# Three modulation vectors a stage later, three by column-group products on TensorE

## The chip, the cores and the metric

One core of one Trainium2 chip runs the whole program. The metric is device time in microseconds (us) of one execution. The engines are TensorE (PE in the profile, its weight loads PEld), VectorE (DVE), ScalarE (ACT), GpSimd (POOL) and the SyncE queue (SP), which issues most transfers.

## The reference, cut to what matters

Two layers of a hybrid backbone run over two streams of 256 tokens each: the latent stream (stream 1 in the kernel) and the context stream (stream 0). Every layer has a SwiGLU FFN, a token mixer of four branches, and a second FFN. Each of these sub-layers is wrapped in a norm with shift, scale and gate vectors, and those are nine columns of 1024 out of one product per layer and stream:

```
mod_l = (act_l @ w_mod[i] + b_mod[i])          # act_l = silu(c),     latent
mod_c = (act_c @ w_mod[i][:, :n_c] + ...)      # act_c = silu(c_ctx), context; last layer: 5 of 9
xl = ffn_sublayer(xl, ml, 0, ...); hl = modulated_norm(xl, g[2], ml[3], ml[4])
xl = xl + ml[5] * rms_norm(yl, g[3]); xl = ffn_sublayer(xl, ml, 6, ...)
```

A modulation vector is a product of one activation row of 1024 with a 1024 x 1024 matrix, 4 MB of weights in float32. Vectors are numbered j = 0 to 8; 0 to 2 belong to the first FFN, 3 to 5 to the mixer, 6 to 8 to the second FFN. A vector has to be there when its sub-layer starts (shift and scale) or ends (gate).

## The kernel before, in words

The program runs in stages: a start (norms of the input, vectors 0 and 1 of layer 0), stage A (first FFN of layer 0), the mixer of layer 0, stage B (second FFN of layer 0), stage C (first FFN of layer 1), the mixer of layer 1, and the last FFN. All large products split each float32 operand in a high and a low part and do three matmuls (`mm3`, L227 to L229).

An FFN stage has 22 rounds of two units. A unit (`unit`) loads a 128x1024 chunk of weights into a `raw` buffer (SP queue), ScalarE makes its high part `wh` (L220), VectorE its low part `wl` (L221), and TensorE does 24 matmuls of 512 columns. There are 4 `raw` buffers and 3 of each part. After the rounds, `outproj` does 16 chunk pairs in two halves (d = 0 with the banks of `psy`, d = 1 with all four banks of `psa`), then six more chunks and the boundary to the next stage.

The remaining modulation vectors are made beside that, tile by tile (128x1024 weights, 8 tiles a vector), by `mod_flow`. A tile is loaded; VectorE multiplies it with one stream's activation row and sums along the row (`jk`, L329). For the other stream GpSimd multiplies in place (L333) and ScalarE sums (L306), one step later. Where layer is 0 and j is at least `JB`, VectorE does both streams and GpSimd and ScalarE none. In layer 1 vectors 5 to 8 have one stream only. A `stepper` is called once for each unit and each chunk pair (60 calls in an FFN stage): after `skip` calls it advances the generators at a fixed rate, (sum of their counts) / total tiles a call.

- Stage A: `stepper([(mod_flow(0, [2, 3, 4], acts0), 25), (mod_flow(0, [5, 6, 7, 8], acts0), 33)], 46, 12)`. Its tiles share the 4 `raw` buffers and the SP queue with the FFN's weights.
- Stage B: vectors 0 to 4 of layer 1, 42 counts over 50 calls, skip 4. Its tiles (`mraw`) have a ring of two buffers of their own and are issued on GpSimd's queue (L298).
- Stage C: vectors 5 to 8 of layer 1, 34 over 50, skip 4, same ring.

Other work fills the same stages. In stage A `setup_s5` builds tables for the state space branch by chains of small operations that go back and forth between GpSimd (L205 to L210, and two powers, L1027 and L1031) and VectorE (L1059 to L1112), at a lowered priority, and `hyena_filters` does some matmuls (psm) and VectorE work. In stages B and C `s5_tables` fills tables of three and five slices on GpSimd and VectorE.

A scheduler orders the instructions of every engine but TensorE when the program is built, by priority and its own estimate of durations, and gives each tile the first buffer of its ring that it expects to be free. TensorE's order is the order of the program text. At run time each engine and queue works strictly in its order.

Of the kernel before, what the change touches and what calls it, by code (L numbers as in the profile page):

```python
# [9 lines left out]
F32 = mybir.dt.float32  # L10
F32R = mybir.dt.float32r
BF16 = mybir.dt.bfloat16
AF = mybir.ActivationFunctionType
ALU = mybir.AluOpType
AX = mybir.AxisListType

P = 128
D = 1024
KT = 8
# [60 lines left out]
RAW0 = 16  # L80
WPF = 2
OW = 1.0
JB = 5


def layout(i):
    i = {k: np.asarray(v) for k, v in i.items()}
    o = {}
# [2 lines left out]
    o["cc"] = np.stack([i["c_ctx"], i["c"][0]])  # L91
    o["wmod"] = i["w_mod"].reshape(L, D, 9, KT, P).transpose(0, 2, 3, 4, 1)
    o["wm1"] = i["w_mod"][0, :, D : 2 * D].reshape(4, 2, P, 2, 512).transpose(3, 0, 2, 1, 4).reshape(2, 4, P, D)
    o["ccf"] = o["cc"].reshape(2, KT, P).transpose(2, 0, 1)
    o["bmod"] = i["b_mod"].reshape(L, 72, P).transpose(0, 2, 1)
    o["ng"] = i["norm_g"].reshape(L, 6, KT, P).transpose(0, 3, 1, 2)
# [15 lines left out]
    w = i["w_in"]  # L112
# [51 lines left out]
def build(tc, A):  # L164
# [20 lines left out]
    with st, tc.manual_schedule(engines={mybir.EngineType.PE}):  # L185
# [99 lines left out]
        def mod_flow(l, js, act, raw=None):  # L285

            if callable(act):
                act = act()  # L290
            tiles = [(j, k) for j in js for k in range(KT)]
            ws, back = {}, []

            def load(n):
                if n < len(tiles):
                    j, k = tiles[n]
                    ws[n] = raw() if raw else rp.tile([P, D], F32, tag="raw", name="raw")
                    (G.dma_start if raw else dma)(ws[n], A["wmod"][l, j, k])  # L298

            def finish():  # L300
                while back:
                    back.pop(0)()

            def sums(w, s, c):
                with after(mark["wh"]):
                    S.activation(w, w, AF.Copy, scale=0.5, accum_out=md[l][:, s, c : c + 1])  # L306

            def bias(j, ss):
                for s in ss:
                    m = md[l][:, s, j * KT : (j + 1) * KT]  # L310
                    V.tensor_tensor(m, m, bmt[l][:, j * KT : (j + 1) * KT], op=ALU.add)

            if raw:
                load(0)
                yield
            for n, (j, k) in enumerate(tiles):
                finish()
                if not raw:
                    load(n)
                c = j * KT + k  # L320
                w = ws.pop(n)
                ss = [1] if l == 1 and j >= 5 else [0, 1]
                both = l == 0 and j >= JB
                fast = ss if both else [1]
                slow = [s for s in ss if s not in fast]
                for s in fast:
                    jk = sp.tile([P, D], BF16, tag="sq", name="jk", bufs=1)
                    with after(mark["wl"]):
                        V.scalar_tensor_tensor(  # L329
                            jk, w, 0.5, act[s], op0=ALU.mult, op1=ALU.mult, accum_out=md[l][:, s, c : c + 1]  # L330
                        )
                for s in slow:
                    G.tensor_tensor(w, w, act[s], op=ALU.mult)  # L333
                    back.append(lambda w=w, s=s, c=c: sums(w, s, c))
                if k == KT - 1:
                    back.append(lambda j=j, ss=ss: bias(j, ss))
                if raw:
                    load(n + 1)
                yield
            finish()  # L340

        def mod_ring(stack, name):

# [311 lines left out]
        class Gates:  # L655
# [5 lines left out]
            def __call__(self, i):  # L661
# [4 lines left out]
                    self.pools.append(pool(self.stack, f"gp{self.name}{n}"))  # L666
                return self.pools[i]

        with ExitStack() as fs:
            with ExitStack() as s0:  # L670
                tp = pool(s0, "start")

                act = [tp.tile([P, D], F32, name=f"act{s}") for s in range(2)]
                acf = tp.tile([P, 2, KT], F32, name="acf")
                dma(acf, A["ccf"])
                acg = tp.tile([P, 2, KT], F32, name="acg")
                S.activation(acg, acf, AF.Tanh, scale=0.5)
# [91 lines left out]
                    f()  # L769
            nxt = {}  # L770
            gp = Gates(fs, "A")
            gp(0)
            with ExitStack() as s1:
                tp5 = pool(s1, "s5s")
# [22 lines left out]
                        acts.extend(act_load())  # L797
                return acts

            st0 = stepper([(mod_flow(0, [2, 3, 4], acts0), 25), (mod_flow(0, [5, 6, 7, 8], acts0), 33)], 46, 12)  # L800

            half = [0]

# [11 lines left out]
        for l in range(L):  # L815
# [8 lines left out]
            with ExitStack() as fs:  # L824
# [4 lines left out]
                else:  # L829
# [3 lines left out]
                        n3.update(coeff=pre_coeff(1, 0, 0, [0, 1]), h=new_h())  # L833

                    x1, raw1 = mod_ring(fs, "mrB")
                    st1 = stepper([(mod_flow(1, [0, 1, 2, 3, 4], act_load, raw1), 42)], 50, 4)
                    tg1 = ahead(fs, gp, "s5p", range(0, 3))

                    def step1(w):
# [5 lines left out]
            if not last:  # L845
                with ExitStack() as fs:
# [4 lines left out]
                        n4.update(coeff=pre_coeff(1, 3, 2, [0, 1]), h=new_h())  # L851

                    x2, raw2 = mod_ring(fs, "mrC")
                    st2 = stepper([(mod_flow(1, [5, 6, 7, 8], act_load, raw2), 34)], 50, 4)
                    tg2 = ahead(fs, gp, "s5q", range(3, 8))

                    def step2(w):
# [44 lines left out]
def hyena_filters(tc, A, hp, psy, Hd, dma, cp, sp, rp, split):  # L902
# [12 lines left out]
    for l in range(L):  # L915
# [37 lines left out]
        for nt in range(2):  # L953
# [9 lines left out]
                f12.append(f)  # L963
            pair = []
            for op in (ALU.add, ALU.subtract):
                su = hp.tile([P, 512], F32, tag="su", name="su", bufs=1)
                V.tensor_tensor(su, f12[0], f12[1], op=op)
                if nt == 0 and op == ALU.add:
                    V.tensor_tensor(su[0:1], su[0:1], hyd, op=ALU.add)
                hi = hp.tile([P, 512], F32R, tag="sh", name="sh", bufs=4)  # L970
                lw = sp.tile([P, 512], F32R, tag="xn", name="sl", bufs=4)
                split(hi, lw, su)
                pair.append((hi, lw))
# [1284 lines left out]
```

## Time and profile before

| what | value |
|---|---|
| three runs, median (lowest to highest) | 2597.41 us (2596.99 to 2599.07) |
| the profiled execution's own time | 2597.24 us |
| its span in the trace | 2595.4 us |
| TensorE busy in the span | 96% |
| VectorE, ScalarE, GpSimd busy | 67%, 42%, 26% |

The span leaves 1.8 us of the execution's own time outside. Busy shares are averages over stages with different limits, so they are read stage by stage: stage A lies at about 60 to 460 us of the span, stage B at 1200 to 1560, stage C at 1590 to 1950. TensorE's matmuls are pipelined: a matmul of 512 columns is shown 390 ns long while the next one starts some 230 ns after it. A waits view says who was waited for; "x" before a number is a count of instructions.

### The profile page before, as it was taken

What the parts mean: (1) busy time and instruction counts of PE and PEld (TensorE: products, weight loads), DVE (VectorE), ACT (ScalarE), POOL (GpSimd) and SP (SyncE); (2) the same over time, 40 slices, a digit from 0 to 9 for tenths busy, and PEclk for the clock granted to TensorE, in tenths of its full rate; (3) what the DMA queues carried; (4) which work ended last, traced back from release to release, by engine and by line L of the source; (5) the groups of instructions that cost most, each with busy time, mean ns of one, the idle gap of its engine ahead of it and who ended that gap; (6) DMA issues with size and microseconds to landing.
All of it is one profiled execution on the core that took longest, in us unless ns stands there. A gap on an engine that the chain in (4) does not pass through costs nothing. (4 is left out here: it accounts for less than half of the span.)

```text
span 2595.4 us, 38077 instructions
## 1 busy us (share of the span) xinstructions
PE 2482.5 (96%) x14606; PEld 2096.0 (81%) x14606; DVE 1750.1 (67%) x2624; ACT 1079.3 (42%) x1828; POOL 671.6 (26%) x692
## 2 busy tenths in 40 slices
PE   6988999999999898999999999999999999998998
PEld 3866888887778776888778888888889889997996
DVE  6888995455645798557998637885435667776664
ACT  5345323454543223434444424332234555355443
POOL 4894000100101784003665403540001012000000
PEclk8999999999999999999999999999999999999999
DMA  6336675223232232343565544676542335865564
GB/s 244 107 118 229 233 256 194 78 82 82 75 109 86 76 97 86 105 159 135 190 213 203 196 162 148 223 239 189 173 138 78 94 111 179 324 227 197 179 192 133
DMA packets 138819, 411.07 MB, mean 158 GB/s; under 512 B 27096, under 2 KB 45321, under 8 KB 135821
## 3 DMA queue, kind: packets, MB, share of 16 engines
q1 hardware_dynamic: 124812, 353.61, 41.8%
q0 software_dynamic: 12672, 45.59, 5.2%
q10 hardware_dynamic: 1152, 9.44, 0.9%
q8 instruction: 115, 1.88, 0.3%
q14 instruction: 68, 0.55, 0.1%
HBM read 374.41 MB, written 34.16 MB: 157 GB/s over the span
## 5 line engine op out<-in xcount | busy, mean ns | idle before, releaser
L221 DVE TENSOR_TENSOR wl<-raw,wh 128x1024 fp32r<-128x1024 f32 x424 | 557.1, 1314 | 468.2 <-ACT wh L220 461.4
L220 ACT ACTIVATE wh<-raw 128x1024 fp32r<-128x1024 f32 x424 | 448.9, 1059 | 748.0 <-issue 184.8
L229 PE MATMUL pin<-hh,wl 128*128 128x512 f32 (+1 forms) x1468 | 529.9, 361 | 18.7 <-DVE wl L221 18.6
L227 PE MATMUL pin<-hh,wh 128*128 128x512 f32 (+1 forms) x1468 | 531.6, 362 | 11.8 <-DVE hh L415 7.8
L228 PE MATMUL pin<-hl,wh 128*128 128x512 f32 (+1 forms) x1468 | 528.7, 360 | 1.7 <-DVE hl L418 1.6
L229 PEld LDWEIGHTS pin<-hh,wl 128*128 128x128 f32 x1468 | 282.5, 192 | 64.7 <-DVE wl L221 24.9
L227 PEld LDWEIGHTS pin<-hh,wh 128*128 128x128 f32 x1468 | 282.8, 193 | 56.9 <-DVE hh L415 9.4
L228 PEld LDWEIGHTS pin<-hl,wh 128*128 128x128 f32 x1468 | 282.6, 193 | 42.7 <-DVE hl L418 3.1
L246 POOL TENSOR_TENSOR r<-v,mhalf 128x1 f32<-128x1 f32 (+2 forms) x46 | 31.4, 682 | 1030.4 <-DVE v L245 931.8
L1345 PE MATMUL pm<-hh,wh 128*128 128x512 f32 (+1 forms) x704 | 251.5, 357 | 0.0
L1347 PE MATMUL pm<-hh,wl 128*128 128x512 f32 (+1 forms) x704 | 245.2, 348 | 0.2 <-DVE wl L221 0.2
L1346 PE MATMUL pm<-hl,wh 128*128 128x512 f32 (+1 forms) x704 | 245.0, 348 | 0.0
L461 PE MATMUL y<-wh,gg 128*128 128x512 f32 x448 | 177.2, 396 | 0.0
L463 PE MATMUL y<-wh,gg 128*128 128x512 f32 x448 | 177.2, 396 | 0.0
L462 PE MATMUL y<-wl,gg 128*128 128x512 f32 x448 | 177.2, 396 | 0.0
L1345 PEld LDWEIGHTS pm<-hh,wh 128*128 128x128 f32 x704 | 134.1, 190 | 18.1 <-issue 2.5
L1347 PEld LDWEIGHTS pm<-hh,wl 128*128 128x128 f32 x704 | 133.8, 190 | 17.8 <-DVE wl L221 0.4
L1346 PEld LDWEIGHTS pm<-hl,wh 128*128 128x128 f32 x704 | 134.1, 191 | 15.0
L329 DVE SCALAR_TENSOR_TENSOR jk<-raw,act 128x1024 bf16<-128x1024 f32 x88 | 117.6, 1336 | 5.0 <-DMA raw<-wmod 4.1
L333 POOL TENSOR_TENSOR mraw<-mraw,act 128x1024 f32<-128x1024 f32 x40 | 102.6, 2565 | 49.6 <-DVE jk L329 48.3
L227 PE MATMUL pm<-hh,wh 128*128 128x256 f32 (+1 forms) x320 | 103.5, 324 | 0.0
L228 PE MATMUL pm<-hl,wh 128*128 128x256 f32 (+1 forms) x320 | 102.7, 321 | 0.1
(481 smaller groups left out, 4933.0 us busy)
## 6 DMA issues: line engine op xcount, KB each, us to landing
raw<-fin SPq DMA_DIRECT2D x176, 512.0 KB, 3.6
raw<-winf SPq DMA_DIRECT2D x122, 512.0 KB, 3.6
mraw<-wmod POOLq DMA_DIRECT2D x72, 512.0 KB, 4.8
raw<-wmod SPq DMA_DIRECT2D x64, 512.0 KB, 4.4
raw<-foa SPq DMA_DIRECT2D x64, 512.0 KB, 3.5
raw<-wbr SPq DMA_DIRECT2D x32, 512.0 KB, 3.6
raw<-fob SPq DMA_DIRECT2D x24, 512.0 KB, 4.1
s5tabd<-rin ACTq DMA_DIRECT2D x8, 1152.0 KB, 7.4
```

What stands on the lines that cost most here:

```text
L220: mark["wh"] = S.activation(wh, w, AF.Copy)
L221: mark["wl"] = V.tensor_tensor(wl, w, wh.bitcast(F32), op=ALU.subtract)
L227: T.matmul(out, lhsT=lh, rhs=rh, start=first and i == 0, stop=False)
L228: T.matmul(out, lhsT=lh, rhs=rl, start=False, stop=False)
L229: T.matmul(out, lhsT=ll, rhs=rh, start=False, stop=last and i == n - 1)
L329: V.scalar_tensor_tensor(jk, w, 0.5, act[s], op0=ALU.mult, op1=ALU.mult, accum_out=md[l][:, s, c : c + 1])
L461: T.matmul(o, lhsT=lh, rhs=rh, start=kt == 0, stop=False)
L462: T.matmul(o, lhsT=lh, rhs=rl, start=False, stop=False)
L463: T.matmul(o, lhsT=ll, rhs=rh, start=False, stop=kt == nk - 1)
L1345: T.matmul(o, lhsT=lh, rhs=rh, start=i == 0, stop=False)
L1346: T.matmul(o, lhsT=lh, rhs=rl, start=False, stop=False)
L1347: T.matmul(o, lhsT=ll, rhs=rh, start=False, stop=i == n - 1)
```

## The change

`JB` rises from 5 to 8. In stage A, `mod_flow` keeps vectors 2 to 4 of layer 0; vectors 5 to 7 are made by a new generator, `mod_pe`, and vector 8 moves to stage B. In stage B the stepper makes vector 8 of layer 0 (both streams on VectorE) and vectors 0 to 2 of layer 1; vectors 3 and 4 of layer 1 move to stage C.

```
-JB = 5
+JB = 8
+    o["wmn"] = i["w_mod"][0, :, 5 * D : 8 * D].reshape(KT, P, 3, D).transpose(2, 0, 1, 3)
+    sel[32 * q + s, q * 2 + s] = 0.5          # q = 0..3, s = 0, 1
+        def mod_pe(tp):
+            sel = tp.tile([P, 8], F32, name="sel")
+            dma(sel, A["sel"])
+            acw = tp.tile([P, KT, 16, 2], F32, name="acw")
+            S.activation(acw, acf....to_broadcast([P, KT, 16, 2]), AF.Copy)
...
+            def turn(j, row):
+                pmt = psa.tile([P, 512], F32, tag="pa", name="pmt")
+                for b in range(2):
+                    T.matmul(pmt[:, 8 * b : 8 * b + 8], lhsT=row[:, b * P : (b + 1) * P], rhs=sel, start=True, stop=True)
+                for s in range(2):
+                    V.tensor_tensor(md[0][:, s, jc]..., pmt[:, 0:16]..., bmt[0][:, jc]..., op=ALU.add)
+            load(0)
+            yield
+            back = []
+            for n in range(3 * KT):
+                j, k = n // KT, n % KT
+                load(n + 1)
+                w = ws.pop(n)
+                if k == 0:
+                    if back:
+                        turn(*back.pop())
+                    row = tp.tile([P, 256], F32, tag="mrow", name="mrow")
+                ps = psa.tile([P, 512], F32, tag="pa", name="psm")[:, :256]
+                for c in range(4):
+                    T.matmul(
+                        ps[32 * c : 32 * c + 32], lhsT=acw[:, k], rhs=w[:, c * 256 : (c + 1) * 256], start=True, stop=True
+                    )
+                with after(mark["wl"]):
+                    if k == 0:
+                        V.tensor_copy(row, ps)
+                    else:
+                        V.tensor_tensor(row, row, ps, op=ALU.add)
+                if k == KT - 1:
+                    back.append((j, row))
+                yield
+            turn(*back.pop())
...
-            st0 = stepper([(mod_flow(0, [2, 3, 4], acts0), 25), (mod_flow(0, [5, 6, 7, 8], acts0), 33)], 46, 12)
+            st0 = stepper([(mod_flow(0, [2, 3, 4], acts0), 25), (mod_pe(mq), 26)], 46, 4)
-                    st1 = stepper([(mod_flow(1, [0, 1, 2, 3, 4], act_load, raw1), 42)], 50, 4)
+                    st1 = stepper([(mod_flow(0, [8], act1, raw1), 10), (mod_flow(1, [0, 1, 2], act1, raw1), 26)], 48, 4)
-                    st2 = stepper([(mod_flow(1, [5, 6, 7, 8], act_load, raw2), 34)], 50, 4)
+                    st2 = stepper([(mod_flow(1, [3, 4, 5, 6, 7, 8], act_load, raw2), 50)], 54, 4)
...
-                su = hp.tile([P, 512], F32, tag="su", name="su", bufs=1)
+                su = sp.tile([P, 512], F32, tag="t", name="su")
```

`mod_pe` holds a weight tile with 128 input channels on the partitions. The activations of both streams, repeated 16 times, are 32 stationary columns; four products of 256 columns each write a group of 32 partitions of one bank. VectorE adds the eight tiles of a vector into `row`; at its end `turn` brings the result to the layout of `md` with two small products. The tiles come from the same 4 `raw` buffers and the SP queue. `acf`, the activations, moves to the pool of constants, and `act1` lets the two generators of stage B share one load of the activation rows. `su`, a tile of the Hyena filters, takes the shared ring `t` in place of a buffer of its own.

## Rows read from the trace of the kernel before

**Rows 1.** The page's first part: busy us, share of the span, instructions.
```profile
PE 2482.5 (96%) x14606; PEld 2096.0 (81%) x14606; DVE 1750.1 (67%) x2624; ACT 1079.3 (42%) x1828; POOL 671.6 (26%) x692
```
**Rows 2.** Stretches of stages A, B, C: length, busy time (count) by engine, granted clock, DMA.
```profile
65.00:128.00 63.00, 61.98 (x298) 50.99 (x297) 53.03 (x133) 25.84 (x34) 54.25 (x65) 1.00 0.34 110
128.00:200.00 72.00, 58.09 (x222) 44.62 (x221) 58.50 (x73) 27.94 (x44) 67.19 (x58) 0.88 0.37 123
200.00:270.00 70.00, 62.05 (x252) 48.47 (x251) 61.48 (x74) 38.19 (x57) 34.52 (x13) 0.95 0.63 225
270.00:330.00 60.00, 60.00 (x266) 49.44 (x265) 57.92 (x95) 21.47 (x30) 0.00 (x0) 1.00 0.70 236
1215.00:1365.00 150.00, 145.35 (x743) 119.25 (x742) 140.81 (x152) 66.27 (x107) 95.06 (x77) 0.99 0.59 198
1610.00:1760.00 150.00, 150.00 (x817) 123.91 (x816) 121.03 (x169) 50.82 (x80) 65.05 (x94) 1.00 0.71 234
```
**Rows 3.** Waits from 128 to 200 us: us in total, times, longest.
```profile
ACT raw L306 <- POOL raw L333: 29.6, 9, 8.8
PE pin L229 <- DVE wl L221: 10.0, 4, 4.0
```
**Rows 4.** Timeline of POOL: start, duration, line, operation.
```profile
77.52 11.09 POOL L1031 TENSOR_TENSOR s5s_er<-s5s_e,s5s_a 128x64 f32<-128x64 f32 x1 [4.95 <-issue]
...
128.37 2.42 POOL L333 TENSOR_TENSOR raw<-raw,act 128x1024 f32<-128x1024 f32 x1
...
194.86 1.20 POOL L210 TENSOR_TENSOR s5ni<-s5ni,s5pt 128x64 f32<-128x64 f32 x1
...
265.90 2.74 POOL L333 TENSOR_TENSOR raw<-raw,act 128x1024 f32<-128x1024 f32 x1 [2.43 <-DVE jk L329]
```
**Rows 5.** Groups by line, POOL, 60 to 460 us: busy us, mean ns, idle before.
```profile
L333 POOL TENSOR_TENSOR raw<-raw,act 128x1024 f32<-128x1024 f32 x24 | 64.3, 2682 | 37.6 <-DVE jk L329 34.0 <-ACT wh L220 2.4 <-ACT raw L306 1.2
```
**Rows 6.** The same, 128 to 200 us.
```profile
L333 POOL TENSOR_TENSOR raw<-raw,act 128x1024 f32<-128x1024 f32 x12 | 31.8, 2650 | 3.5 <-DVE jk L329 3.5
```
**Rows 7.** Timeline of the SP queue in stage A.
```profile
238.34 0.80 SPq L176 DMA_DIRECT2D raw<-wmod  x2
245.41 0.33 SPq L176 DMA_DIRECT2D raw<-fin  x1
```
**Rows 8.** Timeline of PE in the mixer of layer 0.
```profile
892.18 0.40 PE L1347 MATMUL pm<-hh,wl 128*128 128x512 f32 x1
892.51 1.08 PE L2021 MATMUL pn<-vv,bb 64*32 64x128 f32 x32
893.51 0.50 PE L1345 MATMUL pm<-hh,wh 128*128 128x512 f32 x1
893.85 0.40 PE L1346 MATMUL pm<-hl,wh 128*128 128x512 f32 x1
...
903.60 1.09 PE L2048 MATMUL pn<-ident,wt 128*128 128x128 f32 x8
904.45 0.48 PE L1345 MATMUL pm<-brh,wh 128*128 128x512 f32 x1
```
**Rows 9.** Groups by line, DVE, 130 to 270 us.
```profile
L329 DVE SCALAR_TENSOR_TENSOR jk<-raw,act 128x1024 bf16<-128x1024 f32 x21 | 35.2, 1677 | 2.7 <-DMA raw<-wmod 2.6
```
**Rows 10.** The same, 270 to 400 us.
```profile
L329 DVE SCALAR_TENSOR_TENSOR jk<-raw,act 128x1024 bf16<-128x1024 f32 x61 | 74.4, 1220 | 2.2 <-DMA raw<-wmod 1.5
```
**Rows 11.** Groups by line, DVE, 1215 to 1365 us (stage B).
```profile
L221 DVE TENSOR_TENSOR wl<-raw,wh 128x1024 fp32r<-128x1024 f32 x26 | 43.0, 1654 | 2.5 <-ACT wh L220 2.5
```
**Rows 12.** Groups by line, POOL, 1215 to 1365 us.
```profile
L333 POOL TENSOR_TENSOR mraw<-mraw,act 128x1024 f32<-128x1024 f32 x20 | 51.3, 2567 | 31.7 <-DVE jk L329 30.5 <-DVE md L311 1.2
L298 POOL DMA_DIRECT2D mraw<-wmod x19 | 11.3, 595 | 16.6 <-ACT mraw L306 15.2 <-DMA mraw<-wmod 1.5
```
**Rows 13.** Groups by line, DVE, 1615 to 1760 us (stage C).
```profile
L221 DVE TENSOR_TENSOR wl<-raw,wh 128x1024 fp32r<-128x1024 f32 x25 | 33.9, 1356 | 6.7 <-ACT wh L220 6.7
L329 DVE SCALAR_TENSOR_TENSOR jk<-mraw,act 128x1024 bf16<-128x1024 f32 x17 | 21.9, 1286 | 0.0
```

More of the change, by code (lines that the diff above doesn't have):

```diff
@@ L93, in layout @@
     o["wm1"] = i["w_mod"][0, :, D : 2 * D].reshape(4, 2, P, 2, 512).transpose(3, 0, 2, 1, 4).reshape(2, 4, P, D)
+    o["wmn"] = i["w_mod"][0, :, 5 * D : 8 * D].reshape(KT, P, 3, D).transpose(2, 0, 1, 3)
+    sel = np.zeros((P, 8), np.float32)
+    for q in range(4):
+        for s in range(2):
+            sel[32 * q + s, q * 2 + s] = 0.5
+    o["sel"] = sel
     o["ccf"] = o["cc"].reshape(2, KT, P).transpose(2, 0, 1)
@@ L340, in mod_flow, with load @@
             finish()
+        def mod_pe(tp):
+            sel = tp.tile([P, 8], F32, name="sel")
+            dma(sel, A["sel"])
+            acw = tp.tile([P, KT, 16, 2], F32, name="acw")
+            S.activation(acw, acf.rearrange("p s k -> p k s").unsqueeze(2).to_broadcast([P, KT, 16, 2]), AF.Copy)
+            acw = acw.rearrange("p k i s -> p k (i s)")
+            ws = {}
+            def load(n):
+                if n < 3 * KT:
+                    ws[n] = rp.tile([P, D], F32, tag="raw", name="raw")
+                    dma(ws[n], A["wmn"][n // KT, n % KT])
+            def turn(j, row):
+                pmt = psa.tile([P, 512], F32, tag="pa", name="pmt")
+                for b in range(2):
+                    T.matmul(pmt[:, 8 * b : 8 * b + 8], lhsT=row[:, b * P : (b + 1) * P], rhs=sel, start=True, stop=True)
+                jc = slice((5 + j) * KT, (6 + j) * KT)
+                for s in range(2):
+                    V.tensor_tensor(
+                        md[0][:, s, jc].rearrange("p (c b) -> p c b", b=2),
+                        pmt[:, 0:16].rearrange("p (b c s) -> p s c b", b=2, s=2)[:, s],
+                        bmt[0][:, jc].rearrange("p (c b) -> p c b", b=2),
+                        op=ALU.add,
+                    )
[14 more added lines that the diff above has]
+                        ps[32 * c : 32 * c + 32], lhsT=acw[:, k], rhs=w[:, c * 256 : (c + 1) * 256], start=True, stop=True
+                    )
+                with after(mark["wl"]):
[7 more added lines that the diff above has]
+            turn(*back.pop())
         def mod_ring(stack, name):
@@ L667, in __call__ @@
                 return self.pools[i]
+        acf = cp.tile([P, 2, KT], F32, name="acf")
         with ExitStack() as fs:
@@ L771, in build @@
             gp = Gates(fs, "A")
+            mq = pool(fs, "mq")
             gp(0)
@@ L835, in build, with act1 @@
                     x1, raw1 = mod_ring(fs, "mrB")
-                    st1 = stepper([(mod_flow(1, [0, 1, 2, 3, 4], act_load, raw1), 42)], 50, 4)
+                    acts1 = []
+                    def act1():
+                        acts1.extend([] if acts1 else act_load())
+                        return acts1
+                    st1 = stepper([(mod_flow(0, [8], act1, raw1), 10), (mod_flow(1, [0, 1, 2], act1, raw1), 26)], 48, 4)
                     tg1 = ahead(fs, gp, "s5p", range(0, 3))
```

1 line of the change is left out of this document (removed).

## The prediction

> **What bounds the kernel now.** I read the busy shares first, then stretches of the three stages that the change touches, then the waits of the stretch where TensorE is not full. TensorE is busy 96% of the span [rows 1], so a microsecond put on it costs one unless it falls into one of its gaps, and relief of another engine pays only where a gap is. In stage A the full pace stands at 270 to 330 us: 266 matmuls in 60 us, 4.43 per us [rows 2]. VectorE is 97% busy there and nothing is lost. From 128 to 270 us TensorE does 222 + 252 = 474 matmuls [rows 2], at that pace 107 us of work, so 35 us of the 142 are lost: 13.9 + 8.0 = 22 us idle, the rest at the lower granted clock that follows the gaps (0.88 and 0.95). That stretch is the one where vectors 2 to 4 are made: the first multiplication of GpSimd starts at 128.37, the last of 24 at 265.90 [rows 4, 5]. The waits say how: ScalarE waits 29.6 us for GpSimd's product, its weight splits stand behind that in its order, and TensorE waits for `wl` [rows 3]. In the first half GpSimd is 93% busy [rows 2], since the S5 set-up is on it until 196 us [rows 4].
>
> So what VectorE does for vectors 5 to 8 (after 270 us) costs no time now, and that is the work the change removes from it. What matters is what happens to the 35 us, what the products cost on TensorE, and what stages B and C do with the moved vectors.
>
> **The change part by part.** The trace's own time is 2597.24 us (span 2595.4 and 1.8 around it), 0.2 under the median of the three runs; all sums start from 2597.2.
>
> *Removed in stage A.* Vectors 5 to 8 were 32 tiles with two VectorE sums each, 64 x 1.22 us [rows 10] = 78 us of VectorE. They lie beside full TensorE work: gain 0. Nothing on TensorE is late there next.
>
> *Added in stage A: 24 tiles on TensorE.* A tile is four float32 products of 256 columns, each two instructions. Whole-array float32: 8 instructions of 128 columns take 904.45 - 903.60 = 0.85 us [rows 8], 0.106 each, so 0.212 for 256 columns. If the four column groups run side by side, two instructions deep, a tile takes 0.425 us; if not, 8 x 0.212 = 1.70. The nearest row is the block of L2021, four groups of 32 columns: 32 instructions of 128 columns in place of 3.4 us take from 892.51 to 893.51, and the dense matmuls around it lose 893.51 - 892.41 + 0.11 = 1.21 us against their 0.23 us rhythm (0.34 after the block) [rows 8]. Its streaming, eight deep, is 0.85, so 0.36 is entry, exit and weight loads. A tile is then 0.425 + 0.36 = 0.79; with fewer weight loads in it I take 0.75. 24 x 0.75 = 18 us, and three `turn`s of four tiny instructions, at most 0.5 us each by the same rest, 1 us. Sum +19, with ends of +11 (0.43 a tile and no rest) and +51 (1.70 + 0.36). It is on the path: these calls (the 26th to the 49th) come after some 200 us, where TensorE is to be full.
>
> The row shows 0.36 us of loss around each switch between whole-array and grouped products [rows 8]. The Trainium skill, "TensorEngine Tiling (Array Packing)", section "Tiling Modes", says that a change of tiling mode drains TensorE; the trace agrees, by 0.11 us in the first interval after the block alone. By the same page's ideal of 4x, without that, the 24 tiles would be an estimated 10 us.
>
> *New waits.* A product waits for its tile's transfer, for one of four `psa` banks and so for VectorE's addition two or three tiles back, and all later units stand behind it on TensorE. The tile is issued a call ahead and VectorE is 78 us lighter, so I take 0; uncovered, it is up to one late chunk, the 4.0 us of [rows 3], each. The 24 additions and the six small ones of `turn` (256 columns or fewer, against 1.22 us for 1024) lie under TensorE. On SP 24 tile transfers take the place of 24, and eight fewer follow; `sel`, the copy `acw` and `su` in the ring of `t` are beside other work: 0, at most 4 us for `su`.
>
> *Moved: vectors 2 to 4 of stage A start eight calls earlier.* The rate falls from 58/46 = 1.26 tiles a call to 51/46 = 1.11. A call is a unit, 24 x 0.227 = 5.44 us, so a tile is due every 4.91 us instead of 4.31. Now a tile takes (265.90 - 128.37)/23 = 5.98 us [rows 4]; 24 x (5.98 - 4.31) = 40 by this measure stands against the 35 lost. The same 5.98 after gives 24 x (5.98 - 4.91) = 26, and scaled by 35/40, 23 us. From the other side: the tiles will start eight calls earlier, near 128.4 - 8 x 5.44 = 85 us, while GpSimd has the second power in hand (until 88.6) and most of the set-up to do: at most 43 us to 128 and 67.19 - 31.8 = 35.4 after [rows 2, 4, 6], with 24 x 2.68 = 64 [rows 5] together 142 us for 24 tiles due in 118. That is 24 us lost if all of the set-up keeps its place, and near 0 if it all gives way. The calls that bring two tiles, after which the next weight chunk waits 7 us on SP [rows 7], fall from five to three. I take 23: a gain of 12, with ends of 35 (no loss left) and -5 (40 lost, since VectorE at 84% before 128 us [rows 2] gets nine sums of 1.68 us [rows 9] more and is full too).
>
> *Stage B.* It loses 4.65 us idle and, at clock 0.99 over 150 us, 1.5 more: 6 us [rows 2], with VectorE at 94%. GpSimd loses 16 products of 2.57 us [rows 12] (and 16 ScalarE sums); VectorE keeps 40 sums, 16 of them now for vector 8. I take -4, between 0 and -6.
>
> *Stage C.* It loses nothing now. 16 tiles more: VectorE +16 sums, GpSimd +16 products (41 us) and 16 issues of 0.6 us [rows 12]; the rate rises from 0.68 to 0.93 a call. VectorE is at 121 us of 150 [rows 2]; +27.6 calls x 0.25 x 1.29 [rows 13] = 9, and what the products stretch: `wl` takes 1654 ns in B, 1356 in C [rows 11, 13], 25 x 0.3 = 7.5. That is 138 of 150, as in B, so a loss as in B: I take +5, between 0 and +15.
>
> The stretching is in rows: the sums take 1677 ns beside GpSimd's products and 1220 without [rows 9, 10]. The Trainium skill, "SBUF — State Buffer", section "SBUF: two separate sides", says that GpSimd and a VectorE operation with two inputs lock each other out for a whole instruction; the trace agrees in kind, and by the rule at its worst 16 products of 2.57 us would hold VectorE for an estimated 41 us in C.
>
> Sum: +19 - 12 - 4 + 5 = +8, 2605 us.
>
> **The rivals.** *The set-up gives way (faster).* The S5 work has lowered priority; if it falls behind the products and finishes beside `mod_pe`, where VectorE and GpSimd are idle, then the early, slower stepping leaves ScalarE no wait. Place: 85 to 205 us. With 5 us lost instead of 23 the sum is -10, 2587 us. It decides from a loss of 10 us on, 0.4 us a tile: below that the time is faster. For it: GpSimd's product takes 2.4 to 2.7 us [rows 4, 5] of the 4.91 due. Against it: beside the set-up ScalarE waited up to 8.8 us for one such product [rows 3], so the built order does not yield enough at run time; and at 200 to 270, with no set-up, 8 us idle stayed [rows 2].
>
> *The groups do not run side by side.* K is 128 here and 64 in L2021. Then +51 instead of +19: 2637 us. Against it: only the depth differs.
>
> *Stage C runs into GpSimd.* Vectors 3 and 4 are due in 17 calls, 94 us: products 41, issues 10, tables 94 x 65/150 = 41 [rows 2, 12], 92 of 94 us. If the ring of two tiles then holds VectorE's order, and `wl` with it, C loses 15 to 20 instead of 5: 2618 us. Against it: the tables can slip, as none is needed before the next mixer.
>
> *The products cost nothing (the change does not do what it says).* If TensorE keeps gaps at 205 to 330 us, the 19 us fall into them: 2590 to 2600 us. Against it: with VectorE light there is no reason for gaps there.
>
> **How the numbers follow.** A measurement of this kernel tells 0.2%, 5 us, from no change: 2592 to 2603 is "same". Forecast, 2595 to 2616: 45% (10 of it same, 35 slower). Set-up gives way: 28% (24 faster, 4 same). No side-by-side: 7%, slower. Stage C: 13%, slower. Products hidden: 7% (3 faster, 4 same). So faster 0.27, same 0.18, slower 0.55. Time 2605. The range takes in most of the faster case down to 2584 and stage C with a TensorE cost above the row up to 2628; the no-overlap case is left out.
>
> **What would show it.** Right: a block of eight grouped instructions costs 0.7 to 0.8 us of TensorE's rhythm; gaps from about 85 to 205 us, in part where there are none now (65 to 128 has 1 us idle), ScalarE waiting for GpSimd in them; full pace less the blocks from 200 on; VectorE under 60% there; gaps in B smaller, a few us of gaps in C before 1760. Wrong: a full stretch from 65 to 205 us (then faster), blocks of over 1.5 us, or TensorE waits for `raw` from the new weights, which I put at 0.

## The result and the profile after

The changed kernel takes 2678.38 us (median of four runs, 2676.05 to 2683.39); the kernel before, on the same chip, 2598.24. The ratio is 1.0311 [1.0294, 1.0327]: 80 us slower, where 8 were forecast and 2628 was the end of the range.

Where the 80 us are is best seen at the stage ends. The first operation of GpSimd on the next norm (`r<-v,mhalf`) marks each end, in every trace; lengths are differences of these marks, in us. The runs that are explained further down stand here too, so that they can be compared.

| profiled run | stage A | mixer | stage B | stage C | rest of span |
|---|---|---|---|---|---|
| before | 448.9 | 721.2 | 387.1 | 381.7 | 656.5 |
| after | 501.0 | 720.1 | 379.7 | 419.0 | 658.9 |
| early | 470.3 | 721.1 | 385.0 | 383.0 | 658.2 |
| late | 442.8 | 722.7 | 387.2 | 381.9 | 657.1 |
| later | 442.0 | 721.9 | 387.8 | 381.8 | 656.6 |
| pe_first | 461.8 | 720.9 | 410.3 | 382.9 | 659.4 |
| one_pe | 445.4 | 721.5 | 384.9 | 382.7 | 661.1 |
| late_start | 474.6 | 719.3 | 380.7 | 417.6 | 657.9 |
| late_pool | 466.0 | 720.8 | 387.7 | 382.1 | 659.0 |
| twice | 509.7 | 721.7 | 380.3 | 420.4 | 661.5 |
| a_only | 500.9 | 721.6 | 408.3 | 382.1 | 656.9 |
| c_only | 448.1 | 720.5 | 379.5 | 418.4 | 658.2 |
| c_vec | 501.3 | 721.8 | 380.8 | 401.3 | 660.9 |
| c_last | 447.4 | 720.8 | 380.3 | 399.2 | 656.2 |
| c_clear | 448.0 | 721.2 | 378.9 | 401.4 | 658.8 |
| c_clear28 | 452.4 | 725.0 | 379.3 | 395.1 | 657.8 |
| b_clear | 443.2 | 722.0 | 403.3 | 382.7 | 658.0 |
| all_clear | 442.3 | 721.4 | 381.7 | 400.9 | 661.0 |

After against before: A +52.1, mixer -1.1, B -7.4, C +37.3, rest +2.4; together the 83.3 by which the two profiled spans differ (2678.7 and 2595.4). Each row is one trace, and parts whose program is that of before scatter by up to 5 or 6 us: stage A is 447.4 to 452.4 long in c_only, c_last, c_clear and c_clear28, the mixer 719.3 to 725.0 in all rows; the trace of c_clear28 is of an execution 6 us above that kernel's median.

The first part of the page of the changed kernel, beside [rows 1]:
```profile
PE 2518.3 (94%) x14810; PEld 2109.4 (79%) x14810; DVE 1712.6 (64%) x2552; ACT 1081.5 (40%) x1829; POOL 685.9 (26%) x700
```
VectorE has 38 us less work, as meant. GpSimd is busy for 14 us more, though its products are 64 before and after; some 4 of that are eight more issues of transfers. TensorE has 36 us more busy time for 204 more instructions, and its share has still fallen: the rest of the loss is idle time.

The stretches of [rows 2] in stages A and C, after (length, busy time and count by engine, granted clock, DMA):
```profile
65.00:128.00 63.00, 56.03 (x251) 44.95 (x250) 58.45 (x108) 26.64 (x40) 48.08 (x21) 0.92 0.44 143
128.00:200.00 72.00, 59.52 (x234) 46.60 (x233) 63.23 (x89) 30.09 (x45) 66.70 (x63) 0.88 0.40 128
200.00:270.00 70.00, 41.37 (x153) 31.39 (x152) 48.43 (x75) 29.25 (x43) 47.60 (x53) 0.80 0.55 183
270.00:330.00 60.00, 60.00 (x303) 45.33 (x302) 29.08 (x43) 15.44 (x21) 0.00 (x0) 1.00 0.42 142
1610.00:1760.00 150.00, 134.96 (x743) 111.93 (x741) 130.04 (x162) 63.80 (x121) 94.88 (x98) 0.97 0.52 172
```
Stage C starts 44 us later now, so the last stretch lies earlier in its stage than before; the first four compare directly. TensorE is short in the first and, above all, in the third (153 matmuls where 252 stood), and full from 270 us, where the products come. From 85 to 270 us, before and then after:
```profile
85.00:270.00 185.00, 163.14 (x660) 128.06 (x659) 155.52 (x237) 83.78 (x121) 140.90 (x134) 0.94 0.45 153
```
```profile
85.00:270.00 185.00, 137.94 (x527) 106.89 (x526) 151.95 (x246) 77.06 (x112) 147.33 (x132) 0.85 0.46 152
```
At the full pace of 4.43 matmuls per us, 660 are 149 us of work and 527 are 119: 36 us are lost before, 66 after. That is 30 of stage A's 52. The waits of ScalarE in this stretch, before and after (total, times, longest):
```profile
ACT raw L306 <- POOL raw L333: 38.6, 14, 8.8
```
```profile
ACT raw L312 <- POOL raw L339: 57.9, 14, 10.9
```
The timeline of GpSimd after (start, duration) tells why. Against [rows 4] the first product has come forward by 52 us, ahead of the second power, and the last only by 19:
```profile
76.15 2.41 POOL L339 TENSOR_TENSOR raw<-raw,act 128x1024 f32<-128x1024 f32 x1 [3.32 <-DVE jk L335]
...
83.45 11.04 POOL L1097 TENSOR_TENSOR s5s_er<-s5s_e,s5s_a 128x64 f32<-128x64 f32 x1
94.46 7.21 POOL L339 TENSOR_TENSOR raw<-raw,act 128x1024 f32<-128x1024 f32 x3
111.19 2.37 POOL L339 TENSOR_TENSOR raw<-raw,act 128x1024 f32<-128x1024 f32 x1 [9.51 <-DVE s5s_li L1101]
...
247.07 2.34 POOL L339 TENSOR_TENSOR raw<-raw,act 128x1024 f32<-128x1024 f32 x1
```
A tile takes (247.07 - 76.15)/23 = 7.43 us, where 5.98 were taken over from before. The set-up, from which pieces stand between any two products from 113 us on, sends its tables to memory at 246.93 instead of 197.28 (SP's timeline), and that meets a wait which I had not seen. TensorE's longest wait of the stage, and the instruction of ScalarE by which it ends:
```profile
246.93 6.08 SPq L182 DMA_DIRECT2D s5d<-s5tab  x8
```
```profile
PE pin L233 <- DVE t L606: 16.7, 1, 16.7
```
```profile
257.82 1.15 ACT L238 ACTIVATE gg<-t 128x512 fp32r<-128x512 f32 x2 [6.27 <-DMA raw<-wmn]
```
`gg` here is the first gate of round 8. By the program its pool `gp(1)` is opened after the set-up's pool `s5s` is closed and takes its memory, so the gate can't be written before the tables have been read out. The trace names the new weights' transfer for that wait, but the gate begins as the last table lands: issued at 252.5, landed 5.0 to 5.7 us later. The run late_start below names `s5d<-s5tab`. Only the last 6.3 of the 16.7 us are this wait; ahead of it ScalarE stood 5.15 us behind a product of GpSimd.

The products themselves, from TensorE's timeline, beside [rows 8]:
```profile
279.44 0.39 PE L235 MATMUL pin<-hh,wl 128*128 128x512 f32 x1
279.76 0.64 PE L388 MATMUL psm<-raw,acw 128*32 128x256 f32 x8
280.33 0.50 PE L233 MATMUL pin<-hh,wh 128*128 128x512 f32 x1
280.67 0.39 PE L234 MATMUL pin<-hl,wh 128*128 128x512 f32 x1
```
From the last dense matmul ahead to the second behind are 1.23 us; two steps of the rhythm are 0.46, so a block costs 0.77 us, 24 of them 18.5. The first starts at 279.8 us, after the whole loss of 85 to 270: the products can't have made it.

In stage C the waits of 1660 to 1820 us and VectorE's costliest groups of 1700 to 1760 (beside [rows 13]):
```profile
ACT mraw L312 <- POOL mraw L339: 27.3, 11, 6.4
...
DVE jk L335 <- DMA mraw<-wmod: 16.6, 4, 7.8
PE pin L235 <- DVE wl L227: 15.0, 6, 5.2
```
```profile
L227 DVE TENSOR_TENSOR wl<-raw,wh 128x1024 fp32r<-128x1024 f32 x7 | 15.4, 2204 | 0.0
L335 DVE SCALAR_TENSOR_TENSOR jk<-mraw,act 128x1024 bf16<-128x1024 f32 x7 | 11.4, 1622 | 8.8 <-DMA mraw<-wmod 8.8
```
`wl` takes 2204 ns on average, where [rows 13] have 1356; over 1659 to 1804, as far into the stage as [rows 13], it is 1858 for 18 of them. ScalarE waits for products and VectorE for transfers that GpSimd issues between its products and tables.

### The profile page after: what moved, and what is told of

Read it like the earlier page. It is cut to its first block, busy times and chain, and to the rows that moved or that the text cites. A ratio compares the mean times of both kernels' runs of the same rounds, so it can differ in the third digit from the quotient of the medians.

```text
span 2678.7 us, 38416 instructions
## 1 busy us (share of the span) xinstructions
PE 2518.3 (94%) x14810; PEld 2109.4 (79%) x14810; DVE 1712.6 (64%) x2552; ACT 1081.5 (40%) x1829; POOL 685.9 (26%) x700
## 5 line engine op out<-in xcount | busy, mean ns | idle before, releaser
L233 PE MATMUL pin<-hh,wh 128*128 128x512 f32 (+1 forms) x1468 | 537.3, 366 | 33.3 <-DVE t L606 18.7
L335 DVE SCALAR_TENSOR_TENSOR jk<-mraw,act 128x1024 bf16<-128x1024 f32 x88 | 114.3, 1299 | 23.1 <-DMA mraw<-wmod 22.9
```

Source lines behind the costliest of these rows:

```text
L233: T.matmul(out, lhsT=lh, rhs=rh, start=first and i == 0, stop=False)
L335: V.scalar_tensor_tensor(jk, w, 0.5, act[s], op0=ALU.mult, op1=ALU.mult, accum_out=md[l][:, s, c : c + 1])
```

## The experiments

Theory 1, stage A: vectors 2 to 4 begin on top of the S5 set-up, and each engine's order makes the one wait for the other. Rival: the products on TensorE, with their shared buffers. Theory 2, stage C: GpSimd's products of vectors 3 and 4 fall on GpSimd's S5 tables. Rival: six vectors are too many sums for VectorE in one stage. Each ratio is against the kernel before, run on the same chip beside it (2597.95 to 2600.93 us).

**One stage's change alone.** a_only takes stage A from the change and stage C from before; c_only moves vectors 3 and 4 to C and changes nothing else.
```diff
a_only, from after:
-st1 = stepper([(mod_flow(0, [8], act1, raw1), 10), (mod_flow(1, [0, 1, 2], act1, raw1), 26)], 48, 4)
+st1 = stepper([(mod_flow(0, [8], act1, raw1), 10), (mod_flow(1, [0, 1, 2, 3, 4], act1, raw1), 42)], 50, 4)
-st2 = stepper([(mod_flow(1, [3, 4, 5, 6, 7, 8], act_load, raw2), 50)], 54, 4)
+st2 = stepper([(mod_flow(1, [5, 6, 7, 8], act_load, raw2), 34)], 50, 4)
c_only, from before:
-st1 = stepper([(mod_flow(1, [0, 1, 2, 3, 4], act_load, raw1), 42)], 50, 4)
+st1 = stepper([(mod_flow(1, [0, 1, 2], act_load, raw1), 26)], 48, 4)
-st2 = stepper([(mod_flow(1, [5, 6, 7, 8], act_load, raw2), 34)], 50, 4)
+st2 = stepper([(mod_flow(1, [3, 4, 5, 6, 7, 8], act_load, raw2), 50)], 54, 4)
```


> Stage A as in the change (vectors 2 to 4 early, then the products); vector 8 and vectors 0 to 4 of the second layer in stage B, stage C as before. Theory 1 (stage A's loss is the start of vectors 2 to 4 on top of the S5 set-up) and its rival (the products on TensorE make it) both expect stage A about 52 us longer than before, since both are in it. Theory 2 (stage C is lost to two more vectors on GpSimd and VectorE there) expects stage C back at 382 us and the whole at about 2645 to 2655. If the two stages are not independent, the whole is outside that.

> Only the move of vectors 3 and 4 of the second layer from stage B to stage C; stage A as before, no products. Theory 2 expects stage C about 37 us longer and stage B 5 to 8 us shorter, the whole at 2625 to 2635. If stage C suffered from what stage A left behind (clock, late transfers), the whole would be below 2610.


c_only: 2628.84 us, 1.0115 [1.0083, 1.0147]. Stage C +36.7, B -7.6, A as before: the 37 us are stage C's own. a_only: 2674.03, 1.0289 [1.0258, 1.0320]. Stage C is back at 382.1 and A stays at 500.9, yet the whole missed its range, since stage B with six vectors is 21 us longer than before. Six vectors cost a stage dearly in B too.

**No products, but the early start.** One line of the kernel before:
```diff
-st0 = stepper([(mod_flow(0, [2, 3, 4], acts0), 25), (mod_flow(0, [5, 6, 7, 8], acts0), 33)], 46, 12)
+st0 = stepper([(mod_flow(0, [2, 3, 4], acts0), 25), (mod_flow(0, [5, 6, 7, 8], acts0), 33)], 54, 4)
```


> The kernel before with one change of its stage A: the steps of the vectors start at call 5 instead of call 13, at about the rate of the changed kernel; no products on TensorE, no vector moved. Theory 1 expects the stretch from 85 to 270 us to lose about 60 to 66 us instead of the 35 of before, and stage A 15 to 35 us longer, 2613 to 2633 in all. The rival (the products and their buffers make the loss) expects stage A no longer than before, 2590 to 2600.


2618.11 us, 1.0074 [1.0044, 1.0103]; stage A +21.4. From 85 to 270 us, the waits of ScalarE and TensorE there and the table transfers:
```profile
85.00:270.00 185.00, 147.90 (x571) 115.63 (x570) 151.72 (x260) 76.20 (x112) 150.20 (x132) 0.87 0.47 156
```
```profile
ACT raw L306 <- POOL raw L333: 63.7, 16, 9.4
```
```profile
PE pin L227 <- DVE t L547: 12.8, 1, 12.8
```
```profile
239.47 4.69 SPq L176 DMA_DIRECT2D s5d<-s5tab  x8
```
571 matmuls are 129 us: 56 lost, a little under the 60 expected, without one product on TensorE. TensorE waits for the gate of round 8 here too, so neither the products nor `su` in the ring of `t` make that wait. Theory 1 holds, its rival falls, with 20 of the 30 us shown without products.

**The late start.** Three runs push the start away from the set-up: late and later in the kernel before (calls 17 and 19), late_start in the changed kernel (call 13, as before).
```diff
late:        46, 12)  ->  42, 16)      later:  46, 12)  ->  40, 18)
late_start:  46, 4)   ->  40, 12)
```


> The kernel before with one change of its stage A: the steps of the vectors begin at call 17 instead of call 13 and end at the same call (58 steps over 42 calls instead of 46). No products on TensorE, no vector moved. Theory 1 (the loss comes from GpSimd products put over the S5 set-up) expects the set-up to be through by about 160 us, as when the products on TensorE went first (there it was at about 145), the loss of 85 to 270 to fall from 36 us to 10 to 20, some of it to come back later as the steps stand closer; stage A 0 to 25 us shorter, 2573 to 2598 in all. The rival (VectorE and GpSimd have too much work in stage A wherever it stands) expects the same loss later: 2598 to 2615.

> The kernel before with the steps of stage A beginning at call 19 and ending at the same call 58 (58 over 40 calls); beside it the start at call 17 gave 2594 and at call 13 the 2598 of before. If more distance from the set-up is still worth something, 2588 to 2593; if VectorE is the limit of what is left, 2594 to 2600.

> The changed kernel with one edit: stage A's steps begin at call 13, as in the kernel before, instead of call 5, and end at call 52 (51 steps over 40 calls). Products, stages B and C as changed. Theory 1 expects stage A to lose between 85 and 270 us what the kernel before loses there (36 us instead of 66), the products still to cost 18.5 us, and the wait for the set-up's tables to shrink to the few us of before: stage A at 461 to 470 us instead of 501, the whole 2638 to 2648. If something else of the change makes stage A's loss, stage A stays above 490 and the whole above 2667.


late: 2594.26 us, 0.9987 [0.9976, 0.9999]. later: 2593.61, 0.9976 [0.9965, 0.9987], a little faster than both kernels, between its two ranges and not to be told from late. In late the tables go out at 150.66, and ScalarE's wait falls to 15.5 us:
```profile
150.66 4.68 SPq L176 DMA_DIRECT2D s5d<-s5tab  x8
```
```profile
ACT raw L306 <- POOL raw L333: 15.5, 10, 2.7
```
```profile
85.00:270.00 185.00, 168.44 (x697) 134.09 (x696) 160.05 (x236) 86.24 (x124) 120.67 (x133) 0.95 0.46 153
```
697 matmuls are 157 us, so 28 are lost, not the 10 to 20 expected: with the collision gone, most of the loss stays. VectorE is over 22 of 25 us busy in every stretch from 150 to 250. The collision was a part of the loss of before, not all of it; that VectorE makes the rest was not tested.

late_start: 2651.73, 1.0202 [1.0173, 1.0232], 4 us over its range; stage A 474.6, against 501.0 of the change. The start at call 5 instead of 13, with the pace that goes with it, is worth 26 us. From 85 to 270 us, the gate of round 8, and 270 to 330:
```profile
85.00:270.00 185.00, 166.08 (x671) 131.62 (x671) 156.62 (x240) 85.27 (x123) 142.34 (x134) 0.93 0.49 159
```
```profile
210.26 1.16 ACT L238 ACTIVATE gg<-t 128x512 fp32r<-128x512 f32 x2 [1.44 <-DMA s5d<-s5tab]
```
```profile
270.00:330.00 60.00, 54.06 (x277) 39.31 (x276) 26.53 (x46) 16.63 (x23) 0.00 (x0) 0.99 0.56 187
```
671 matmuls leave 34 us lost, as before the change. Stage A is 5 us over the expected 470: TensorE idles 6 us from 270 to 330, where the products come closer together than in the change, and ScalarE waits 26.3 us for its weights' transfers. The gate of round 8 begins 12.4 us after the issue of the table transfers (197.88); in the change it was 10.9, in early 9.1, in before 12.6. In before and in the change too it begins as the last table lands; in early the tables had landed by 246.7, and the gate, at 248.57, came right behind a sum for which ScalarE had waited 3.7 us. No run gave the set-up memory of its own, so the deadline is read from the program and these traces, not tested.

**The products first, or only one of them.** pe_first makes the products from call 1, during the set-up, vectors 2 to 4 after them; its stages B and C are those of a_only. one_pe makes vector 8 alone on TensorE, then 2 to 7 as before.
```diff
pe_first, from a_only:
-st0 = stepper([(mod_flow(0, [2, 3, 4], acts0), 25), (mod_pe(mq), 26)], 46, 4)
+st0 = stepper([(mod_pe(mq), 26), (mod_flow(0, [2, 3, 4], acts0), 25)], 44, 0)
one_pe (JB = 5, mod_pe with one vector; B and C as before):
+st0 = stepper([(mod_pe(mq), 10), (mod_flow(0, [2, 3, 4], acts0), 25), (mod_flow(0, [5, 6, 7], acts0), 25)], 50, 8)
```


> Products on TensorE first, from call 1, while GpSimd makes the S5 set-up; vectors 2 to 4 after them, at about call 23; stage B with vector 8 and vectors 0 to 4 of the second layer, stage C as before. Theory 1 expects the S5 set-up to end at least as early as before and no wait of TensorE for it; the products still cost their 18.5 us, and the lost time of 85 to 270 falls from 66 to below 35: stage A between 10 us shorter and 20 us longer than before, the whole 2590 to 2622. The rival (products on TensorE make the loss through the shared buffers) expects stage A at least 45 us longer, 2640 or more.

> Stage A: vector 8 alone by column-group products on TensorE, from call 9; then vectors 2 to 4 and 5 to 7 on GpSimd and VectorE as in the kernel before, from about call 17. Stages B and C as before. Theory 1 expects the set-up to run through undisturbed, 8 blocks to cost 8 x 0.77 = 6.2 us, and VectorE to be relieved of 8 tiles (some 45 us of its time) near the end of the stage: stage A 5 to 20 us shorter, 2578 to 2593 in all. The rival (the products themselves disturb stage A) expects stage A longer than before by the 6 us and more: 2604 or above.


pe_first: 2634.54 us, 1.0137 [1.0105, 1.0169], over its range because of stage B's +23 with six vectors. Stage A is as theory 1 wants: +12.9, with the tables out at 149.28 and ScalarE's wait at 14.7 us. a_only and this run, which differ only in the order and the start of the two generators, are 39 us apart in stage A. one_pe: 2597.94, 0.9997 [0.9986, 1.0008]; stage A -3.5, less than the 5 to 20 expected and no more than stage A scatters by itself. Neither case of its expectation came.

**The products twice.** Each product is issued a second time over the same bank.
```diff
-for c in range(4):
+for c in (0, 1, 2, 3, 0, 1, 2, 3):
     T.matmul(ps[32 * c : 32 * c + 32], lhsT=acw[:, k], rhs=w[:, c * 256 : (c + 1) * 256], start=True, stop=True)
```


> The changed kernel with every product on TensorE issued twice (the second time over the same bank, same sum): 24 blocks of 16 instructions in place of 8. If the blocks stand on the path and their entry is paid once a block, each grows by the 0.43 us that four groups side by side need, and the whole by 10 us: 2688. If each product costs its whole price again, by 18.5: 2697. If they lie beside other work, nothing: 2678. If the groups do not run side by side, by 24 x 1.70 = 41: 2719.


```profile
278.13 0.39 PE L235 MATMUL pin<-hh,wl 128*128 128x512 f32 x1
278.44 1.07 PE L388 MATMUL psm<-raw,acw 128*32 128x256 f32 x16
279.45 0.50 PE L233 MATMUL pin<-hh,wh 128*128 128x512 f32 x1
279.79 0.40 PE L234 MATMUL pin<-hl,wh 128*128 128x512 f32 x1
```
The block grows from 1.23 to 1.66 us, by the 0.43 of four groups side by side; entry and exit (0.77 - 0.43 = 0.34) are paid once. Stage A grows by 8.7 against 24 x 0.43 = 10.3, so the blocks are on the path. The whole grew by more, to 2695.19 us, 1.0370 [1.0340, 1.0400], which by itself is nearer to the 2697 of the second case; the block and stage A decide for the first. Some 6 us of the growth lie behind stage A, 0.6 to 2.6 in each part, no more than such parts scatter.

**GpSimd for more of it.** The first stream of vectors 5 to 8 goes to GpSimd, idle there in the kernel before.
```diff
later ->  JB = 5  ->  JB = 9
```


> The kernel before with the steps of stage A beginning at call 19 (58 over 40 calls) and the first stream of vectors 5 to 8 on GpSimd, which is idle from 270 us on in the kernel before, instead of VectorE. No products on TensorE, no vector moved. If the remaining loss of stage A after the later start is VectorE's work, 32 tiles x 1.22 = 39 us less of it lets stage A become 10 to 25 us shorter than before: 2573 to 2588. If GpSimd's products hold VectorE and ScalarE up wherever they stand, stage A is as long as before or longer: 2598 to 2615.


2618.81 us, 1.0076 [1.0047, 1.0105]: the second case, 4 us over its range, with stage A 24 us longer than in later. 270 to 440 us and VectorE's two large groups there, in this run and then in later, which differs in `JB` alone:
```profile
270.00:440.00 170.00, 148.48 (x619) 115.55 (x618) 141.76 (x141) 74.23 (x114) 91.99 (x34) 0.99 0.60 210
```
```profile
L329 DVE SCALAR_TENSOR_TENSOR jk<-raw,act 128x1024 bf16<-128x1024 f32 x34 | 61.7, 1815 | 2.7 <-DMA raw<-wmod 2.6
L221 DVE TENSOR_TENSOR wl<-raw,wh 128x1024 fp32r<-128x1024 f32 x25 | 44.8, 1793 | 19.5 <-ACT wh L220 19.5
```
```profile
270.00:440.00 170.00, 166.61 (x717) 133.48 (x715) 139.69 (x215) 49.72 (x60) 5.17 (x2) 1.00 0.74 244
```
```profile
L329 DVE SCALAR_TENSOR_TENSOR jk<-raw,act 128x1024 bf16<-128x1024 f32 x66 | 80.5, 1219 | 1.1 <-DMA raw<-wmod 0.3
L221 DVE TENSOR_TENSOR wl<-raw,wh 128x1024 fp32r<-128x1024 f32 x30 | 36.6, 1221 | 14.0 <-ACT wh L220 14.0
```
32 sums fewer save VectorE nothing (139.69 and 141.76 us busy): the instructions that are left take half as long again on average, and TensorE loses 18 us in a stretch that was nearly full. With no set-up near, GpSimd's products cost by themselves. 34 of them stretch 34 sums and 25 `wl` by 0.60 and 0.57 us, some 35 us.

**Stage C.** c_vec is the change with the first stream of vectors 3 and 4 on VectorE, so no GpSimd product. The others are c_only with another order or a later start.
```diff
c_vec, from after:
-both = l == 0 and j >= JB
+both = l == 0 and j >= JB or l == 1 and 3 <= j < 5
from c_only's stage C, [3, 4, 5, 6, 7, 8], 54, 4:
c_last:     [5, 6, 7, 8, 3, 4], 44, 0
c_clear:    [3, 4, 5, 6, 7, 8], 34, 24
c_clear28:  [3, 4, 5, 6, 7, 8], 30, 28
```


> The changed kernel with one edit: the first stream of vectors 3 and 4 of the second layer is also summed on VectorE, so that no GpSimd product stands in stage C; VectorE gets 16 more sums of about 1.2 us, 20 us of work. If the GpSimd products over the tables make stage C's loss, it falls from 37 to below 15 us: 2640 to 2657 in all. If VectorE has too much work, stage C becomes longer than 419: 2680 or more.

> Stage C takes vectors 3 and 4 of the second layer as in the change, but after vectors 5 to 8 instead of before them, so that their GpSimd products come when the S5 tables of GpSimd are through (about 1760 us); stage B with vectors 0 to 2, stage A as before. If stage C's 37 us are GpSimd products over GpSimd's tables, stage C is at most 10 us longer than the 382 of before, and with stage B's 8 us saved the whole is 2585 to 2602. If six vectors are too much for VectorE in stage C wherever they stand, stage C stays 25 us or more longer: 2615 or above.

> Only the move of vectors 3 and 4 of the second layer to stage C, as in c_only, but stage C's steps begin at call 25 instead of call 5 (50 over 34 calls), when the S5 tables are nearly through. If the loss is the place beside the tables, stage C is at most 10 us longer than the 382 of before and the whole 2588 to 2602. If six vectors are too many sums for one stage, their closer steps keep 20 us or more of the loss: 2612 or above.

> The same with stage C's steps from call 29 (50 over 30 calls), wholly after the tables. By place: as c_clear or a few us less, 2586 to 2600. By number: more than c_clear, since the steps stand closer still.


Stage C over before: c_only +36.7, c_vec +19.6, c_last +17.5, c_clear +19.7, c_clear28 +13.4 (medians 2667.25, 1.0270 [1.0240, 1.0300]; 2609.87, 1.0053 [1.0034, 1.0073]; 2610.16, 1.0041 [1.0025, 1.0058]; 2605.44, 1.0018 [1.0007, 1.0029]). Of the last four none met either end in time; c_clear28 is 5 us under c_clear, as it was to be by place. Without the products, or with them clear of the tables, about half of the loss goes: that half is the collision. c_vec has 16 VectorE sums more than the change and its stage C is 17.7 us shorter, so the number of VectorE's sums alone does not make the loss. The other 13 to 20 us stay in all four runs; that they come from six vectors in one stage is argued by what is left, and no run shows it by itself. 1640 to 1760 us in c_only and in before, then 1840 to 1960 in c_clear28, with VectorE's wait:
```profile
1640.00:1760.00 120.00, 96.21 (x462) 75.65 (x461) 101.91 (x112) 41.03 (x70) 81.73 (x81) 0.89 0.57 190
```
```profile
1640.00:1760.00 120.00, 120.00 (x654) 99.12 (x653) 97.90 (x141) 41.49 (x65) 51.43 (x74) 1.00 0.74 246
```
```profile
1840.00:1960.00 120.00, 112.29 (x465) 88.19 (x464) 73.03 (x107) 29.05 (x37) 16.50 (x32) 0.97 0.73 255
```
```profile
DVE jk L329 <- DMA mraw<-wmod: 31.6, 22, 2.7
```
VectorE in c_only does 112 instructions in the time of 141, in a little more busy time; GpSimd has 30 us more (its stage C begins 9 us earlier than in before). In c_clear28 the tables' stretch is full, and TensorE is idle for 8 us later, where the steps stand closer and each sum waits for its transfer, 22 times. What part of the rest is those transfers and what the ring's order stays open.

**The same distance in stage B, and everywhere.** b_clear is later with stage B from call 17; all_clear is later with B's three vectors from call 13 and C as in c_clear.
```diff
b_clear:    later + [0, 1, 2, 3, 4], 50, 4  ->  38, 16
all_clear:  later + [0, 1, 2], 32, 12  and  [3, 4, 5, 6, 7, 8], 34, 24
```


> The kernel before with stage A's steps from call 19 (as in later, 2593.6) and stage B's five vectors from call 17 instead of call 5 (42 over 38 calls). Stage B's tables of GpSimd run in its first half; before, TensorE lacks some 12 us of 1180 to 1340. If the same distance helps there, 2580 to 2590; if stage B's loss is its start and not the vectors, 2592 to 2597.

> All three stages: A from call 19, B with vectors 0 to 2 from call 13, C with vectors 3 to 8 from call 25; no products on TensorE. If the move to stage C is worth stage B's 7 us once its sums keep clear of the tables, 2580 to 2592; if stage C keeps a loss, 2600 or above.


b_clear: 2611.11 us, 1.0045 [1.0028, 1.0062], a miss of both cases. Stage B from call 17 is 16 us longer (403.3). From 1340 to 1560 us ScalarE waits 110.5 us for GpSimd's products there, against 28.2 in about the same stretch of before (1349 to 1554), where TensorE is full. In c_clear28 it is VectorE that waits, for transfers; common to both is that the steps stand closer. all_clear: 2609.25, 1.0027 [1.0009, 1.0044], its second case, since stage C keeps 19 us of loss and A and B give back 12. With the vectors that a stage had before, the later start is a gain only in stage A; with six vectors in stage C it takes back 17 (c_clear) and 23 us (c_clear28) of c_only's 37.

## Why the prediction was wrong

*Products on TensorE, +19: right.* 24 x 0.77 = 18.5 us, by the block of the trace, side by side and with a switch of 0.34 us a block; twice shows both parts. The rivals of no overlap and of free products fall.

The switch is in the rows: 0.34 us a block here, 0.36 in [rows 8]. The Trainium skill, "TensorEngine Tiling (Array Packing)", section "Tiling Modes", says that a change of the tiling mode drains TensorE; the traces agree, and twice adds that a longer block pays it once.

*Removed in stage A, 0: right.* From 270 to 440 us TensorE is busy for 170.00 of 170 us before and 168.63 after.

*Moved: vectors 2 to 4 start earlier, -12: this step failed.* It measured +30 in 85 to 270 us (66 lost, 36 before). The step put the time of a tile at 5.98 us, taken from a stretch where half the set-up was done, and let the slower rate absorb it; its bound added up GpSimd's work (142 us in 118) as if only the sum counted. What counts is the order on three engines: a product waits for a piece of set-up, ScalarE's weight split for the product, the set-up for the next product. GpSimd was busy 147 us where it had been 141, but a tile took 7.43. early (+21.4, no products), late_start (-26.4) and pe_first (39 us by order and start alone) show that the place makes the loss; the chain itself is read from the waits, and no run tells the order apart from the stretching that the last section shows.

*New waits, 0: wrong, at a place that I had not looked at.* Not the weights or the banks, but the first gate of round 8, 16.7 us of TensorE, the last 6.3 for memory that the late set-up still held; a wait of 8.7 us at 143.72 for VectorE's part of the filters (`psm`; 8.5 in early) was in no term either. Both are within the 30. The deadline also speaks against the rival "the set-up gives way", which wanted the set-up to finish beside `mod_pe`, after it. ScalarE's wait for it was in the trace of before, equally long and put down to another transfer; TensorE waited 4.0 us there, at 212.52, for the `wh` that ScalarE makes behind that gate:
```profile
209.89 1.15 ACT L232 ACTIVATE gg<-t 128x512 fp32r<-128x512 f32 x2 [6.21 <-DMA raw<-fin]
```

*The condition of the loss before.* The 35 us were put down to the collision. late shows that 28 stay without it, under a VectorE that is over 90% busy in every stretch of 150 to 270; that it is the cause is not shown.

*Stage B, -4: right in sign, -7.4 measured*, a little over the end of 6.

*Stage C, +5 (0 to 15): mis-sized; +37.3.* The term scaled the stretch of `wl` from stage B and counted VectorE's sum at 138 of 150 us. The rival "stage C runs into GpSimd" named the place and put 15 to 20 on it; c_vec and c_last put the products' share at 18 to 19, so that was its price, but the other 13 to 20, put down to six vectors in one stage because nothing else is left, were in no term. Adding up VectorE's work could not show it: in c_only VectorE is busy for 101.91 of 120 us while TensorE is idle for 24.

With what was measured the sum is +18.5 + 30 - 7.4 + 37.3 = +78, beside the 80 of the runs. Of stage A's 52 us 3 to 4 are in neither term. By TensorE's timeline the three `turn`s, forecast at 1 us, cost some 2 of them (one waits 0.84 us for VectorE's last addition); for the rest I have no cause. That the change is slower had the larger chance, 55%, but on the cost of the products, which alone is 18.5 us; the other 60 come from the two terms that failed.

## What to carry to other kernels

When a step is moved earlier, look at what else its engine must finish there and who waits for that, memory that is to be reused among it; work that adds up to less than the time still loses it when three engines serve each other in order. A trace shows a deadline as a short wait long before it is expensive: follow each such wait to what ended it. GpSimd relieves VectorE only where the two do not meet; before counting the sums saved, look at how long single VectorE instructions take beside a product, not only at the mean.

## What the runs showed of the hardware

Moving 32 of 66 sums from VectorE to GpSimd left VectorE's busy time at some 140 us (139.69 in later, 141.76 in late_pool); I had expected 39 us of relief. The mean of 1815 ns hides two cases. Of the 59 sums and splits of late_pool from 270 to 440 us, 39 take 1.21 to 1.23 us, as without products. The other 20 take 2.02 to 3.45, and each of them overlaps a product and ends 1.07 to 1.09 us after that product's end. Two of them, GpSimd and then VectorE:
```profile
338.46 2.73 POOL L333 TENSOR_TENSOR raw<-raw,act 128x1024 f32<-128x1024 f32 x1 [2.35 <-DVE jk L329]
342.41 2.37 POOL L333 TENSOR_TENSOR raw<-raw,act 128x1024 f32<-128x1024 f32 x1 [1.22 <-issue]
```
```profile
338.85 3.41 DVE L329 SCALAR_TENSOR_TENSOR jk<-raw,act 128x1024 bf16<-128x1024 f32 x1
342.72 3.14 DVE L221 TENSOR_TENSOR wl<-raw,wh 128x1024 fp32r<-128x1024 f32 x1 [0.45 <-ACT wh L220]
```
So VectorE stands until the product is over and then does most of its work (1.07 of 1.21 us); a product that starts inside a VectorE instruction takes 3.3 to 3.4 us in place of 2.4. The Trainium skill, "SBUF — State Buffer", section "SBUF: two separate sides", says that GpSimd and a VectorE operation with two inputs exclude each other for a whole instruction. The trace agrees. The 1.0 us of VectorE per product of 2.70 us is an average over those that met and those that did not.

Eight products in four column groups cost 0.77 us between dense matmuls, sixteen 1.20: 0.43 a pass and 0.34 for the change of mode.
